# Even layer: the value sums of two query tiles of a head pair in one step behind the scores, and exponentials written over their arguments

## The chip, the cores and the metric

One core of a Trainium2 chip runs the whole kernel. The metric is the device time of one execution in microseconds (us); the median of the runs is given, with the lowest and the highest.

## The reference

The reference is a two-layer encoder over 256 tokens of 1024 features. Each layer is a mixer and a squared-ReLU MLP, each behind an RMS norm and with a residual. The even layer's mixer has two groups of 8 heads, which share an input projection and an output projection:

```python
hcat = xn @ w_in
out_a = neighbourhood_attention(...)        # 8 heads of 64, bias rpb, windows of a 64-wide grid
...
out_b = dense_attention(q, k, v, (MLA_NOPE + MLA_ROPE) ** -0.5)   # 8 heads, queries and keys of 96, values of 64
return jnp.concatenate([out_a, out_b], axis=-1) @ w_o
```

For each head and each query, both compute the softmax of the scores against all 256 keys and the weighted sum of the values. The odd layer (three dilated windows) and the MLPs are untouched by the change.

## The kernel before

Tokens are two tiles of 128 queries (`NT = 2`). Products that need full precision are made of three matmuls each (`mm3`, lines 208 to 211): an operand is split into a rounded high part, which ScalarE writes (`split`, line 205), and the remainder, which VectorE writes (line 206).

In the even layer, attention is cut into 16 items, in the order neighbourhood heads, then latent heads: for each pair of heads `hp` the query tiles `t = 0` and `t = 1`. So items 2·hp and 2·hp+1 are the two tiles of one pair of heads. An item passes through three steps.

- `scores(n)` (line 773) starts the load of a bias for item n+2, makes the scores of one query tile against 256 keys for two heads on TensorE (`two_heads`, line 218, for the neighbourhood heads, with weights of 64 rows x 128 columns; `mm3` with 96 rows for the latent heads), and computes the softmax: VectorE writes the negated arguments `sn` and their minima (line 791 or 794), ScalarE the exponentials `pp` and their sums (line 796), VectorE the reciprocals (line 797), ScalarE scales `pp` (line 799).
- `turn_probs(n)` (line 802) transposes `pp` in four pieces of 128x128 on TensorE (line 806), and copies the result to `pts` (line 808) on ScalarE or VectorE, whichever the framework takes.
- `mix(n)` (line 810) multiplies `pts` by the values on TensorE: 8 matmuls with weights of 128 rows x 64 columns (line 820), and splits the 128x128 result into the inputs of the output projection, `oah`/`oal` or `obh`/`obl` (lines 205 and 206).

`sn`, `pp` and `pts` come from one ring of 12 scratch buffers, which other parts of the kernel use as well.

The work around these steps is the `main` list: the projections of queries and keys, and, when those are through, the output projection into four open accumulators (`out_steps`; the last two of its eight parts are in `out_last`, behind the list). Each main step has a cost written by hand; the costs, less 5 at the start, add up to 36.3 units. The list of the attention's steps (`attention`, line 824) is spread over these units evenly, by its length:

```python
        for c, f in main:
            f()
            at += c
            while done < len(side) and done * total < at * len(side):
                side[done]()
                done += 1
```

Before the change the list has 50 entries, of which two are empty. From item 2 on its order is `scores(n)`, `turn_probs(n-1)`, `mix(n-2)`, and each is an entry of its own.

The order in which the steps are issued is a priority. The framework's scheduler fixes each engine's order ahead of the run; it keeps to the priorities as long as it expects an instruction's inputs in time, and otherwise lets later ones pass. What an engine is then given, it does in that order.

Weights come from HBM through SyncE's queue (line 151) into four raw buffers, in an order written out ahead (`specs`); the bias loads (line 771) stand in the same queue. Behind the even layer, `hand_over` adds the accumulators to the residual (line 308) and prepares the MLP's input `xx` (lines 245 and 246).

Of the kernel before, what the change touches and what calls it, by code (L numbers as in the profile page):

```python
# [26 lines left out]
P = 128  # L27
D = 1024
KT = D // P
T = 256  # L30
NT = T // P
# [18 lines left out]
def trunk(ctx, tc, a, out):  # L50
    nc = tc.nc
# [8 lines left out]
    def scratch(shape, name):  # L60

        n = int(np.prod(shape))
        v = work.tile([P, 512], F32, tag="scratch", name=name, bufs=12)[:, :n]
        if len(shape) == 2:
            v = v.rearrange("p (a b) -> p a b", b=shape[1])
        return v
# [8 lines left out]
    def quarter_pair(name):  # L75
        return [act.tile([P, KT // 2, T], F32R, tag="quarter", name=name + v, bufs=4) for v in "hl"]

    def bank(tag):
        return ps.tile([P, 512], F32, tag=tag, name=tag)
# [124 lines left out]
    def split(hi, lo, src, eng=None):  # L204
        a = nc.scalar.copy(hi, src).ins  # L205
        return a, (eng or nc.vector).tensor_tensor(lo, src, hi.bitcast(F32), op=ALU.subtract).ins  # L206

    def mm3(o, sh, sl, mh, ml, first, last):
        nc.tensor.matmul(o, sh, mh, start=first, stop=False)  # L209
        nc.tensor.matmul(o, sh, ml, start=False, stop=False)  # L210
        nc.tensor.matmul(o, sl, mh, start=False, stop=last)  # L211

    def two_heads(o, hi, lo, ts):

        for n, (y, z) in enumerate(((hi, hi), (hi, lo), (lo, hi))):
            for j in range(2):
                pb = slice(64 * j, 64 * j + 64)
                nc.tensor.matmul(o[j], y[pb, 0, ts], z[pb, 1, :], start=n == 0, stop=n == 2)  # L218
# [10 lines left out]
    def tok(t):  # L229
        return slice(t * P, (t + 1) * P)  # L230
# [323 lines left out]
    def even(ep):  # L554
# [208 lines left out]
        mixed = [quarter_pair("oa"), None]  # L763
        items = [(0, t, hp) for hp in range(4) for t in range(NT)] + [(1, t, hp) for hp in range(4) for t in range(NT)]
        biases, probs, turned = {}, {}, {}

        def load_bias(n):
            if n < 8:
                _, t, hp = items[n]
                biases[n] = ep.tile([P, 2, T], F32, tag="bias", name="bias", bufs=2)  # L770
                nc.sync.dma_start(biases[n], a["rpb"][t, hp])

        def scores(n):
            kind, t, hp = items[n]
            load_bias(n + 2)

            sb = [bank("w")[:, 0:T] for _ in range(2)] if kind == 0 else bank("w").rearrange("p (j n) -> p j n", j=2)
            s_of = lambda j: sb[j] if kind == 0 else sb[:, j]
            if kind == 0:
                two_heads(sb, *qk[hp], tok(t))  # L780
            else:
                for j in range(2):
                    h = 2 * hp + j
                    (qh, ql), (kh, kl) = mT["q"], mT["k"]
                    mm3(sb[:, j], qh[0:96, h, tok(t)], ql[0:96, h, tok(t)], kh[0:96, h, :], kl[0:96, h, :], True, True)
            pp, sn = scratch([2, T], "pp"), scratch([2, T], "sn")
            mn, z, rz = (work.tile([P, 2], F32, tag=v, name=v, bufs=3) for v in ("mn", "z", "rz"))
            for j in range(2):
                o = s_of(j)
                if kind == 0:  # L790
                    nc.vector.tensor_tensor_reduce(out=sn[:, j], in0=o, in1=biases[n][:, j, :], op0=ALU.add, op1=ALU.min,
                                                   scale=-1.0, scalar=3e38, accum_out=mn[:, j:j + 1])
                else:
                    nc.vector.tensor_scalar(sn[:, j], o, -MLA_SCALE, None, ALU.mult, ALU.min, accum_out=mn[:, j:j + 1])
            for j in range(2):
                nc.scalar.activation(pp[:, j], sn[:, j], AF.Exp, bias=mn[:, j:j + 1], scale=-1.0, accum_out=z[:, j:j + 1])
            nc.vector.reciprocal(rz, z)
            for j in range(2):
                nc.scalar.activation(pp[:, j], pp[:, j], AF.Copy, scale=rz[:, j:j + 1])
            probs[n] = pp  # L800
# [7 lines left out]
            nc.any.tensor_copy(out=turned[n], in_=pt.rearrange("p (b n) -> p b n", b=4))  # L808

        def mix(n):  # L810
            kind, t, hp = items[n]
            pts = turned.pop(n)
            if mixed[kind] is None:
                mixed[kind] = quarter_pair("ob")
            v = (vna, vml)[kind]
            pvo = bank("acc" if n < 6 else "w")
            for kk in range(NT):
                for j in range(2):
                    h = 2 * hp + j
                    nc.tensor.matmul(pvo[64 * j:64 * j + 64, 0:P], v[:, kk, h * 64:(h + 1) * 64], pts[:, 2 * j + kk, :],  # L820
                                     start=kk == 0, stop=kk == NT - 1)
            split(*(z[:, hp, tok(t)] for z in mixed[kind]), pvo[:, 0:P])

        def attention():

            out = []
            for n in range(len(items) + 2):
                for fn, m in ((scores, n), (turn_probs, n - 1), (mix, n - 2)):
                    if 0 <= m < len(items):
                        out.append(lambda fn=fn, m=m: fn(m))  # L830
                if n == 0:
                    out += [lambda: None] * 2
            return out
# [21 lines left out]
        main += [(0, lambda: accs.extend(open_accs()))]  # L855
        main += [(1.3, f) for k in range(6) for f in out_steps(accs, mixed, wo, k)]
        side = attention()
        at = -5
        total = sum(c for c, _ in main) + at
# [296 lines left out]
```

## Time and profile before

| what | value |
|---|---|
| median of 3 runs | 737.01 us (734.08 to 737.18) |
| the profiled execution: its time | 735.7 us |
| its span, first to last instruction | 733.9 us |
| its granted TensorE clock, mean | 0.997 of full speed |
| TensorE matmuls busy | 99% of the span |
| TensorE weight loads busy | 90% |
| VectorE busy | 85% |
| ScalarE busy | 71% |

Busy time counts a matmul from its start to its modelled end, and matmuls overlap, so 99% doesn't say how densely they stand. For that, one reads the distance from one start to the next. In the rows, PE is TensorE's matmuls, PEld its weight loads, DVE VectorE, ACT ScalarE, SPq SyncE's queue.

### The profile page before, as it was taken

To read this page: it belongs to the slowest core of one execution; us is meant where nothing else is said; L and a number is where in the kernel's file an instruction comes from. 1 tells how busy PE (TensorE), PEld (TensorE's weight loads), DVE (VectorE), ACT (ScalarE), POOL (GpSimd) and SP (SyncE) were. 2 spreads that over 40 slices of the span, in tenths; PEclk is the share of its full clock that TensorE was granted. 3 is DMA by queue.
4 is the path that set the end of the run, shared out by engine and by line. 5 is a ranking of instruction groups with operands and counts; after the bars stand their busy time and mean duration, and the time that the engine had idled before them with its cause. 6 is when DMAs were issued, how large, how long until landed. Compare 5 with 4: busy or idle time off the path is not lost.

```text
span 733.9 us, 13862 instructions
## 1 busy us (share of the span) xinstructions
PE 723.2 (99%) x5234; PEld 660.5 (90%) x5234; DVE 623.0 (85%) x1182; ACT 522.5 (71%) x991; POOL 118.4 (16%) x157
## 2 busy tenths in 40 slices
PE   9999999999999999999999999999999999999995
PEld 6988899999999998989899899898999999999984
DVE  6888859999999959878878887787859999999956
ACT  7778968767766756877776767767759766866751
POOL 0100002224222000012213212032103232212000
PEclk9999999999999999999999999999999999999998
DMA  8773338798899644663565555555658799888601
GB/s 314 272 260 138 116 115 215 213 291 241 262 264 241 215 155 166 218 217 126 201 215 184 175 189 184 175 187 202 226 182 214 223 287 258 247 239 252 204 11 57
DMA packets 36867, 149.56 MB, mean 204 GB/s; under 512 B 5120, under 2 KB 6656, under 8 KB 27712
## 3 DMA queue, kind: packets, MB, share of 16 engines
q1 hardware_dynamic: 26208, 128.20, 49.4%
q0 software_dynamic: 10304, 20.19, 15.1%
q8 instruction: 41, 0.67, 0.4%
q10 hardware_dynamic: 288, 0.28, 0.1%
q14 instruction: 26, 0.21, 0.1%
HBM read 142.10 MB, written 1.05 MB: 195 GB/s over the span
## 4 chain that ended last, share of the span: by engine, by line
PE 92%; DVE 4%; issue 1%; ACT 1%; DMA 0%; POOL 0%; POOLq 0%; SPq 0%; ACTq 0%; DVEq 0%
PE w L209 11%; PE w L210 11%; PE w L211 11%; PE acc L209 11%; PE acc L927 11%; PE acc L210 11%; PE acc L211 11%; PE acc L928 5%; PE w L1004 1%; PE w L218 1%; PE w L806 1%; PE acc L1019 1%; DVE wlo L206 1%; PE w L820 1%; DVE xx L246 1%
## 5 line engine op out<-in xcount | busy, mean ns | idle before, releaser
L206 DVE TENSOR_TENSOR wlo<-raw,whi 128x512 fp32r<-128x512 f32 (+3 forms) x360 | 297.8, 850 | 41.3 <-ACT whi L205 41.2
L205 ACT CAST whi<-raw 128x512 fp32r<-128x512 f32 (+3 forms) x360 | 253.9, 747 | 90.0 <-PE w L210 71.0
L210 PE MATMUL w<-xx,whi 128*128 128x256 f32 x528 | 149.6, 283 | 0.4 <-DVE xx L246 0.3
L211 PE MATMUL w<-xx,wlo 128*128 128x256 f32 x528 | 149.3, 283 | 0.0
L209 PE MATMUL w<-xx,whi 128*128 128x256 f32 x528 | 148.8, 283 | 0.0
L927 PE MATMUL acc<-xx,whi 128*128 128x512 f32 x336 | 122.0, 403 | 0.0
L210 PEld LDWEIGHTS w<-xx,whi 128*128 128x128 f32 x528 | 101.2, 192 | 1.9 <-DVE xx L246 0.8
L209 PEld LDWEIGHTS w<-xx,whi 128*128 128x128 f32 x528 | 101.0, 192 | 1.1
L211 PEld LDWEIGHTS w<-xx,wlo 128*128 128x128 f32 x528 | 101.2, 192 | 0.0
L928 PE MATMUL acc<-xx,wlo 128*128 128x256 f32 x336 | 94.3, 281 | 0.0
L144 POOL COPY sum<-sum 128x512 f32<-128x512 f32 x28 | 40.3, 1455 | 244.3 <-DMA sum<-in_w 150.2
L927 PEld LDWEIGHTS acc<-xx,whi 128*128 128x128 f32 x336 | 63.1, 188 | 14.1
L942 POOL DMA_DIRECT2D sw<-qk x84 | 41.4, 500 | 176.7 <-DVE qk L935 167.4
L928 PEld LDWEIGHTS acc<-xx,wlo 128*128 128x128 f32 x336 | 63.5, 189 | 0.0
L209 PE MATMUL acc<-whi,xx 128*128 128x384 f32 (+2 forms) x160 | 55.7, 350 | 0.1
L210 PE MATMUL acc<-wlo,xx 128*128 128x384 f32 (+2 forms) x160 | 55.4, 346 | 0.0
L211 PE MATMUL acc<-whi,xx 128*128 128x384 f32 (+2 forms) x160 | 54.9, 343 | 0.0
L209 PE MATMUL w<-whi,hh 128*128 128x512 f32 (+1 forms) x108 | 42.1, 390 | 0.0
L210 PE MATMUL w<-wlo,hh 128*128 128x512 f32 (+1 forms) x108 | 41.5, 384 | 0.0
L211 PE MATMUL w<-whi,hl 128*128 128x512 f32 (+1 forms) x108 | 41.2, 382 | 0.0
L205 ACT CAST hh<-h 128x896 fp32r<-128x896 f32 (+1 forms) x32 | 28.9, 903 | 14.3 <-DVE h L382 14.2
L206 DVE TENSOR_TENSOR suml<-sum,sumh 128x1024 fp32r<-128x1024 f32 x28 | 35.3, 1259 | 0.0
(233 smaller groups left out, 1576.7 us busy)
## 6 DMA issues: line engine op xcount, KB each, us to landing
raw<-in_w SPq DMA_DIRECT2D x36, 1024.0 KB, 5.2
raw<-in_w_oqk SPq DMA_DIRECT2D x24, 1024.0 KB, 4.9
raw<-in_w SPq DMA_DIRECT2D x28, 768.0 KB, 4.9
sum<-in_w POOLq DMA_DIRECT2D x28, 512.0 KB, 8.8
raw<-in_w_ov SPq DMA_DIRECT2D x16, 768.0 KB, 4.4
sum<-in_w SPq DMA_DIRECT2D x28, 256.0 KB, 6.3
sw<-qk POOLq DMA_DIRECT2D x84, 64.0 KB, 3.2
raw<-in_w_oe SPq DMA_DIRECT2D x4, 1024.0 KB, 5.0
```

Of the source, the lines that this page charges most:

```text
L144: nc.gpsimd.tensor_copy(out=sums[:, 1, :], in_=sums[:, 0, :])
L205: a = nc.scalar.copy(hi, src).ins
L206: return a, (eng or nc.vector).tensor_tensor(lo, src, hi.bitcast(F32), op=ALU.subtract).ins
L209: nc.tensor.matmul(o, sh, mh, start=first, stop=False)
L210: nc.tensor.matmul(o, sh, ml, start=False, stop=False)
L211: nc.tensor.matmul(o, sl, mh, start=False, stop=last)
L218: nc.tensor.matmul(o[j], y[pb, 0, ts], z[pb, 1, :], start=n == 0, stop=n == 2)
L246: lambda: nc.vector.scalar_tensor_tensor(lo, v, gk, hi.bitcast(F32), ALU.mult, ALU.subtract).ins)
L806: nc.tensor.transpose(pt[:, b * P:(b + 1) * P], pp[:, b // 2, (b % 2) * P:(b % 2 + 1) * P], ident)
L927: nc.tensor.matmul(two(pq), wh[:, ws], xT[:, :, k, :], start=k == 0, stop=False)
L928: nc.tensor.matmul(pq[:, T:2 * T], wl[:, ws], xh[:, k, :], start=False, stop=k == KT - 1)
L942: swap = (lambda o, i: nc.gpsimd.dma_start(o, i)) if wide else nc.scalar.copy
```

## The change

`scores` keeps the negated arguments and the exponentials in one buffer. `mix` is called once for two items, with the odd one's number: it takes the transposed probabilities of both query tiles, makes 16 matmuls into one bank of 256 columns, and splits 128x256 at once. In the attention's list, `mix(n-2)` is no longer an entry of its own: for odd n it stands in the entry of `scores(n)`, right behind it and ahead of `turn_probs(n-1)`. The list has 35 entries then, two of them empty.

```diff
-            pp, sn = scratch([2, T], "pp"), scratch([2, T], "sn")
+            pp = sn = scratch([2, T], "pp")
...
         def mix(n):
-            kind, t, hp = items[n]
-            pts = turned.pop(n)
+
+            kind, _, hp = items[n]
             if mixed[kind] is None:
                 mixed[kind] = quarter_pair("ob")
             v = (vna, vml)[kind]
             pvo = bank("acc" if n < 6 else "w")
-            for kk in range(NT):
-                for j in range(2):
-                    h = 2 * hp + j
-                    nc.tensor.matmul(pvo[64 * j:64 * j + 64, 0:P], v[:, kk, h * 64:(h + 1) * 64], pts[:, 2 * j + kk, :],
-                                     start=kk == 0, stop=kk == NT - 1)
-            split(*(z[:, hp, tok(t)] for z in mixed[kind]), pvo[:, 0:P])
+            for t in range(NT):
+                pts = turned.pop(n - 1 + t)
+                for kk in range(NT):
+                    for j in range(2):
+                        h = 2 * hp + j
+                        nc.tensor.matmul(pvo[64 * j:64 * j + 64, tok(t)], v[:, kk, h * 64:(h + 1) * 64], pts[:, 2 * j + kk, :],
+                                         start=kk == 0, stop=kk == NT - 1)
+            split(*(z[:, hp, :] for z in mixed[kind]), pvo[:, 0:T])
 
         def attention():
 
             out = []
             for n in range(len(items) + 2):
-                for fn, m in ((scores, n), (turn_probs, n - 1), (mix, n - 2)):
-                    if 0 <= m < len(items):
-                        out.append(lambda fn=fn, m=m: fn(m))
+
+                now = [(scores, n)] + [(mix, n - 2)] * (n % 2 and n > 2)
+                for step in (now, [(turn_probs, n - 1)]):
+                    step = [(fn, m) for fn, m in step if 0 <= m < len(items)]
+                    if step:
+                        out.append(lambda step=step: [fn(m) for fn, m in step])
                 if n == 0:
                     out += [lambda: None] * 2
             return out
```

## Rows read from the trace of the kernel before

**Rows 1.** The page's first part: busy time, share of span, instructions of each engine.
```profile
PE 723.2 (99%) x5234; PEld 660.5 (90%) x5234; DVE 623.0 (85%) x1182; ACT 522.5 (71%) x991; POOL 118.4 (16%) x157
```

**Rows 2.** Busy time by stretch: window, length, each engine's busy us, clock, DMA, GB/s.
```profile
38.00:112.00 74.00, 74.00 (x629) 65.42 (x628) 57.45 (x175) 59.20 (x164) 3.07 (x6) 1.00 0.44 153
...
60.00:82.00 22.00, 22.00 (x178) 18.84 (x177) 20.03 (x67) 20.41 (x60) 0.89 (x3) 1.00 0.19 61
```

**Rows 3.** Waits of the weight loads, 38 to 112 us: total us, times, longest.
```profile
PEld w L820 <- DVE sn L794: 0.5, 3, 0.2
```

**Rows 4.** Timeline of PE, item 15's sum: start us, us, line, tiles, shape, count.
```profile
107.68 0.28 PE L210 MATMUL acc<-obl,whi 128*128 128x256 f32 x1
...
108.88 0.28 PE L211 MATMUL acc<-obh,wlo 128*128 128x256 f32 x1
109.08 0.66 PE L820 MATMUL w<-pts,vml 128*64 128x128 f32 x8
...
109.89 0.28 PE L210 MATMUL acc<-obl,whi 128*128 128x256 f32 x1
```

**Rows 5.** The same sum in narrow windows, from its second and third pair.
```profile
109.25 0.49 PE L820 MATMUL w<-pts,vml 128*64 128x128 f32 x5
...
109.35 0.39 PE L820 MATMUL w<-pts,vml 128*64 128x128 f32 x4
```

**Rows 6.** Timeline of PE: item 1's sum beside item 4's scores.
```profile
52.95 0.28 PE L211 MATMUL acc<-xx,wlo 128*128 128x256 f32 x1
53.16 0.66 PE L820 MATMUL acc<-pts,vna 128*64 128x128 f32 x8
...
54.51 0.28 PE L210 MATMUL acc<-xx,whi 128*128 128x256 f32 x1
```

**Rows 7.** Timeline of PE: item 1's scores alone, between projections.
```profile
42.93 0.28 PE L211 MATMUL acc<-xx,wlo 128*128 128x256 f32 x1
...
43.91 0.28 PE L210 MATMUL acc<-xx,whi 128*128 128x256 f32 x1
```

**Rows 8.** Timeline of PE: latent scores of item 13 behind the output projection.
```profile
93.23 0.28 PE L211 MATMUL acc<-oah,wlo 128*128 128x256 f32 x1
93.36 0.28 PE L209 MATMUL w<-kh,qh 96*128 96x256 f32 x1
```

**Rows 9.** Timeline of PE: item 8's sum, whose first piece has two matmuls.
```profile
83.51 0.43 PE L820 MATMUL w<-pts,vml 128*64 128x128 f32 x2
```

**Rows 10.** Timelines: transposes of items 15 and 7, and the copies that follow them.
```profile
106.34 0.60 PE L806 MATMUL w<-ident,pp 128*128 128x128 f32 x4
...
106.97 0.59 ACT L808 COPY pts<-w 128x512 f32<-128x512 f32 x1 [0.95 <-PE w L806]
...
72.85 0.60 PE L806 MATMUL w<-ident,pp 128*128 128x128 f32 x4
...
77.11 0.68 DVE L808 COPY pts<-w 128x512 f32<-128x512 f32 x1
```

**Rows 11.** Groups by line, 38 to 112 us: shapes, count, busy us, mean ns, idle.
```profile
L205 ACT CAST obh<-w 128x128 fp32r<-128x128 f32 x8 | 2.1, 261 | 0.9 <-PE w L820 0.8
...
L752 ACT COPY ktok<-acc 128x256 f32<-128x256 f32 x4 | 1.4, 359 | 0.0
...
L206 DVE TENSOR_TENSOR obl<-w,obh 128x128 fp32r<-128x128 f32 x8 | 2.3, 288 | 3.6 <-ACT obh L205 3.5
...
L754 DVE COPY vml<-acc 128x256 f32<-128x256 f32 x4 | 1.7, 420 | 0.4 <-ACT ktok L752 0.3
```

**Rows 12.** The chain that ended last, at the layer's end: start us, us, what.
```profile
109.08 1.06 ACT whi L205
...
111.38 0.20 DVE obl L206
...
119.23 0.39 PE w L210
```

**Rows 13.** Timeline of SyncE's queue: start us, time the issue took, count.
```profile
62.98 40.52 SPq L151 DMA_DIRECT2D raw<-in_w  x5
```

## The prediction

> **What bounds the kernel.** I read the page's busy shares first: TensorE's matmuls fill 99% of the span, VectorE 85%, ScalarE 71% [rows 1]. As overlapping matmuls flatter that share, I then read the changed stretch, 38 to 112 us, by windows: TensorE never shows a gap there, while VectorE and ScalarE have 16.6 and 14.8 us to spare of 74, though in its middle, 60 to 82 us, only 2.0 and 1.6 of 22 [rows 2]. The waits say how much TensorE stands still for others: its longest wait for another engine ahead of a sum of values is 0.5 us in all [rows 3]. So in this stretch the time is the number of TensorE's starts, times their distances; the work of the other engines costs nothing as long as it is in time. That makes the timeline of TensorE's starts the view that decides.
>
> **The distances.** Plain 256-column matmuls start 0.12 us apart: 1.20 us from 107.68 to 108.88 with ten steps [rows 4]. The pairs of a sum start about 0.11 apart once it runs [rows 5]. From the last matmul ahead of the sum of item 15 to the second behind it are 109.89 − 108.88 = 1.01 us [rows 4]. Two plain steps and four pairs would be 0.24 + 0.44 = 0.68. The other 0.33 us is the way in and out: the array goes from weights of 128x128 to 128x64 and back, the first start comes late, the one after it too, and the same again behind the sum.
>
> Scores of neighbourhood heads have such a price as well: 43.91 − 42.93 = 0.98, less 0.24 and three pairs of 0.12, is 0.38 [rows 7]. Where sum and scores stand side by side they share: 54.51 − 52.95 = 1.56, less 0.24, 0.44 and 0.36, is 0.52 [rows 6]. There the sum adds only 0.52 − 0.38 = 0.14. The latent heads' scores, with 96 rows, have no such price: they start 0.13 behind the matmul ahead [rows 8]. So a sum beside them pays its 0.33.
>
> The timeline has 17 pieces of sums in the 16 items, as item 8's is in two [rows 9]: 3 beside neighbourhood scores, 14 not. That is 3 × 0.14 + 14 × 0.33 = 5.04 us.
>
> **What the change does to that.** *Half as many sums.* The matmuls stay as many; a joined sum is 0.44 + 0.44 long and pays its way in and out once. There are 8. Three stand behind neighbourhood scores (items 1, 3 and 5, behind the scores of 3, 5 and 7), five elsewhere: 3 × 0.14 + 5 × 0.33 = 2.07 us. Gain 5.04 − 2.07 = 2.97 us, all of it on TensorE, the engine that bounds. The trace has sums ahead of scores and none behind them; the price there lies between 0 and 0.33, and I take 0.14, as it is the same passage the other way round. If all three cost 0.33 the gain is 2.40.
>
> *Joined sums may come apart.* The scheduler parted item 8's, where one copy was late [rows 9]. Each parting gives back 0.33. I count one of the eight; the bounds are none and all eight, which would leave 0.33 of the gain.
>
> *Splits of 256 columns.* ScalarE's part takes 0.26 us at 128 columns and 0.36 in the nearest copy of 256; VectorE's 0.29 and 0.42 [rows 11]. Eight pairs give 8 × (0.52 − 0.36) = 1.3 us on ScalarE and 8 × (0.58 − 0.42) = 1.3 on VectorE. TensorE hides both, so I count nothing; should the cover go, they are a gain in any case. The Trainium skill, in TensorEngine Tiling (Array Packing), section PSUM Bottleneck, holds that small array forms speed up TensorE but not the reading of its results, and advises to read several tiles of a bank at once. By that rule the gain would be these 1.3 us in place of the 2.97; the short waits of TensorE speak against it here [rows 3].
>
> *Exponentials in place.* No instruction is added or removed; ScalarE reads and writes the same elements in order. Sixteen buffers fewer are drawn from the ring of 12, while the copy of an even item is held until its partner's sum. Nothing on TensorE waited visibly for this ring: no cost, no gain. If buffers became short instead, the copies would be late, which is the rival below.
>
> *The steps' places.* With 35 entries over 36.3 units in place of 50, an entry comes every 1.04 units, not 0.73; a main step of 1.3 units is 12 × 0.12 = 1.44 us. Scores of item 2 move from 3.6 to 5.2 units, those of 15 from 31.9 to 32.2. The bias loads, issued with the scores, move with them, up to 1.8 us later, and the weight loads behind them in SyncE's queue too. That queue spreads the next five weight loads over 40.5 us [rows 13]: it waits for free buffers and is far ahead. No cost; without that lead it would be the 1.8 us at most. GpSimd's queue has nothing of these steps.
>
> *The end of the layer.* The last sum now holds two items: 0.44 us longer, and its split by 0.10 and 0.13. From there the chain goes over VectorE to the next layer's first products at 119.23 [rows 12], so lateness there is not hidden by itself. But the split waited between two weight splits anyway, 0.20 us of it on the chain. Bounds: 0 and 0.67. I take 0.2, nearer to the row's 0.13 of VectorE.
>
> **The sum.** 2.97 − 0.33 − 0.2 = 2.4 us less. The profiled execution took 735.7 (span 733.9 and 1.8 around it), which gives 733.3; the median of the runs shown is 1.3 higher, 737.0, which gives **734.6 us**. That is 0.33% less, under the 0.5% (3.7 us) that a measurement of this kernel can tell from no change.
>
> **Rivals.** *TensorE waits behind the scores* (slower). The sum of an odd item used to come about four entries behind its transposes; now it comes one entry and the scores behind them. By the costs in the code, that is between scores alone (item 13: 0.44 + six matmuls, 0.72, = 1.2 us) and a main step more (2.6). A prompt copy lands 107.56 − 106.34 = 1.2 us after its transposes start, but item 7's landed 77.79 − 72.85 = 4.9 after them, in the crowded middle [rows 10]. There the new distance is 0.44 + about 1.1 + 0.72 = 2.3: 2.6 us late. One such wait nearly cancels the gain; two are 5.2 us, giving 734.6 + 5.2 = 739.8. From 2.4 us of waits on, the change loses. For it: the 2.0 and 1.6 us of room in the middle. Against: the scheduler lets other matmuls pass a sum that it expects late, as in item 8, and both engines have 1.3 us less to do. The Trainium skill, in TensorE: Matmul & The Clock Gate, section Part 3: Packing small matmuls, has it that matmuls run strictly in order; by that rule all that stands behind a waiting sum waits too. Chance 0.12.
>
> *The joining does not reach TensorE.* If the scheduler parts most sums, or moves them away from the scores, the gain shrinks to between 0.33 and 1.3, less 0.2 at the end: about 736.4. For it: one of 16 was parted in a stretch with the copies four entries ahead. Chance 0.18.
>
> *The end of the layer takes it back.* If the next products wait for VectorE's chain, and it starts later by all of 0.67 us plus one weight split of 1.2 that slips ahead, 1.9 us of 2.6 go: 736.3. The gap that the chain shows at its end speaks for it, VectorE's idle time ahead of 109 us against. Chance 0.10.
>
> *More than counted.* If the lighter middle also mends later places in the fixed order, 1 to 2 us come on top: 733. The waits show nothing to mend [rows 3]. Chance 0.10.
>
> **How the numbers follow.** The forecast has the other 0.50, with its own range of 733.4 to 735.4 (no parting and no end cost, 2.97, and up to a slack of 1.6, with the three passages at full price and the end at its bound). The range takes in the rivals between and much of the slower one, and the runs' own 3 us of scatter: 731.8 to 738.6. Faster by over 0.5% is below 733.3: part of the last rival and of the forecast's scatter, 0.15. Slower, above 740.7: the slower rival with more than two waits, 0.06. Same: 0.79.
>
> **What would show it.** Right: 128 matmuls at line 820 as before, but in 8 blocks of 16; about 1.45 us from the matmul ahead of a block to the second one behind it; 8 roundings and 8 subtractions fewer, those left at 256 columns; no wait at line 820 over 0.5 us; the last sum's end about 2.5 us earlier. Wrong: more than 11 blocks; idle time ahead of line 820 of 2.4 us or more; or the last sum earlier but the first products of the next layer not.

## The result, and where the time went

The changed kernel takes 737.21 us, the median of 20 executions (734.99 to 738.50); the kernel before, on the same chip, 735.25 (734.08 to 738.31, 20 executions). The ratio is 1.0021, with an interval of 1.0012 to 1.0030: some 1.5 us more, where 2.4 us less had been forecast. The profiled execution of the changed kernel took 736.64 us, with a span of 734.8 and a mean granted clock of 0.996.

**The even layer does what was forecast.** The page's first part of the changed kernel stands against [rows 1]: nine VectorE and seven ScalarE instructions fewer, as many matmuls.

```profile
PE 720.8 (98%) x5234; PEld 660.2 (90%) x5234; DVE 619.2 (84%) x1173; ACT 520.9 (71%) x984; POOL 123.5 (17%) x157
```

The windows of the stretch (columns as in [rows 2]) show TensorE without a gap, as before, and 17 more starts of matmuls within the same 74 us:

```profile
38.00:112.00 74.00, 74.00 (x646) 67.50 (x645) 56.89 (x168) 58.66 (x158) 3.48 (x7) 1.00 0.46 158
60.00:82.00 22.00, 22.00 (x183) 19.10 (x180) 19.35 (x65) 20.24 (x57) 0.59 (x2) 1.00 0.18 61
```

The timeline of TensorE in the changed kernel at its last sum answers to [rows 4] (the sum is line 822 now):

```profile
106.01 0.28 PE L211 MATMUL acc<-obh,wlo 128*128 128x256 f32 x1
106.22 1.09 PE L822 MATMUL w<-pts,vml 128*64 128x128 f32 x16
107.24 0.39 PE L209 MATMUL acc<-obh,whi 128*128 128x256 f32 x1
107.47 0.28 PE L210 MATMUL acc<-obl,whi 128*128 128x256 f32 x1
```

From the matmul ahead to the second one behind are 107.47 − 106.01 = 1.46 us, and the matmul behind the sum starts at 107.24, not at 109.67. Five of the eight joined sums stand whole like this one. The other three are parted, one of them into three pieces, as the same view shows in the crowded middle:

```profile
64.39 0.66 PE L822 MATMUL acc<-pts,vna 128*64 128x128 f32 x8
...
67.75 0.43 PE L822 MATMUL acc<-pts,vna 128*64 128x128 f32 x2
...
69.24 0.65 PE L822 MATMUL acc<-pts,vna 128*64 128x128 f32 x6
```

That makes 12 pieces in place of 17. Among the next layer's first products TensorE is ahead: the matmul that started at 122.11 us starts at 119.60. Of these 2.5 us it had 0.3 already where the layer begins (39.74 in place of 40.08); the layer itself is 2.2 shorter.

**The lead is lost at one place, 60 us later.** Counting matmuls from the end, the lead is the same for each up to the one that started at 180.34 in the kernel before. The timelines of TensorE at this place, before and then after:

```profile
180.34 0.39 PE L211 MATMUL acc<-sumh,hl 128*128 128x512 f32 x1
180.56 0.28 PE L209 MATMUL w<-xx,whi 128*128 128x256 f32 x1
```
```profile
177.83 0.39 PE L211 MATMUL acc<-sumh,hl 128*128 128x512 f32 x1
180.83 0.39 PE L209 MATMUL w<-xx,whi 128*128 128x256 f32 x1 [2.61 <-ACT relu L373]
```

A distance of 0.22 us has become 3.00. TensorE arrives 2.5 us early and leaves 0.27 late. This is the first MLP. The waits of the changed kernel from 150 to 182 us (columns: who waited for whom, total us, times, longest) name the chain:

```profile
POOL sum L144 <- DVE every L180: 10.1, 1, 10.1
DVE raw L179 <- issue: 7.3, 1, 7.3
...
PEld w L209 <- ACT relu L373: 3.0, 1, 3.0
PE w L209 <- ACT relu L373: 2.6, 1, 2.6
```

Read from below: TensorE waits for ScalarE's `relu`, and VectorE had stood idle for 7.3 us ahead of `raw` (line 179). "issue" means that the view found no releaser there; the timelines do. Here is GpSimd in the changed kernel, then in the kernel before (start, duration):

```profile
155.00 9.70 POOL L144 COPY sum<-sum 128x512 f32<-128x512 f32 x1 [10.12 <-DVE every L180]
165.00 1.09 POOL L145 DMA_DIRECT2D sum<-in_w  x1 [0.30 <-POOL sum L144]
```
```profile
151.93 0.61 POOL L144 COPY sum<-sum 128x512 f32<-128x512 f32 x1 [3.81 <-ACT hh L205]
...
163.01 1.32 POOL L144 COPY sum<-sum 128x512 f32<-128x512 f32 x1 [9.09 <-DMA sum<-in_w]
...
173.17 4.35 POOL L144 COPY sum<-sum 128x512 f32<-128x512 f32 x1 [7.45 <-DVE wlo L206]
```

The MLP's weights come in blocks that are also needed as sums. `load_weight` loads one block (line 143), GpSimd copies it (line 144), and a DMA from GpSimd's queue adds two other blocks to the pair (line 145). The copy takes 0.61 us when it runs freely; here it took 9.70. VectorE's timeline over the same time shows why its row stopped:

```profile
163.55 0.68 DVE L180 TENSOR_TENSOR every<-raw 128x512 f32<-128x512 f32 x1
171.51 0.69 DVE L179 TENSOR_TENSOR raw<-sum,raw 128x512 f32<-128x512 f32 x1 [7.28 <-issue]
```

VectorE ran without a pause until 164.23. It stopped because its next operation needs the block whose copy could not run beside it. Then the copy ended (164.70), the adding DMA went out at 165.00 and had landed by 171.51, and all that hangs on it (`wlo`, `relu`, TensorE's products) came late.

VectorE's row is itself another one. Counted from the end of the kernel, 16 of VectorE's places (121 to 159 us) and 13 of ScalarE's (121 to 149) hold another instruction than before. VectorE's timelines where the long difference begins, before and then after:

```profile
144.45 0.69 DVE L179 TENSOR_TENSOR raw<-sum,raw 128x512 f32<-128x512 f32 x1
145.05 1.22 DVE L206 TENSOR_TENSOR suml<-sum,sumh 128x1024 fp32r<-128x1024 f32 x1
```
```profile
142.94 1.10 DVE L179 TENSOR_TENSOR raw<-sum,raw 128x512 f32<-128x512 f32 x1
143.96 1.22 DVE L206 TENSOR_TENSOR wlo<-raw,whi 128x1024 fp32r<-128x1024 f32 x1
```

So: 2.5 us gained, 2.8 lost. In this profile another 0.65 us went in the odd layer, at a transpose that waited 0.9 us, behind a late transfer; e3, the same kernel, doesn't have that. What probably makes the difference of the medians as large as it is, e3 shows. The chain that ended last (the page's fourth part) has the shift in its shares: 92% for PE and none for POOL before, and now

```profile
PE 77%; DVE 9%; ACT 4%; DMA 4%; issue 3%; POOL 3%; SPq 0%; POOLq 0%; DVEq 0%; ACTq 0%
```

### The profile page after: what moved, and what is told of

Same layout as the page of the kernel before. It is cut to its first block, busy times and chain, and to the rows that moved or that the text cites. A ratio compares the mean times of both kernels' runs of the same rounds, so it can differ in the third digit from the quotient of the medians.

```text
span 734.8 us, 13840 instructions
## 1 busy us (share of the span) xinstructions
PE 720.8 (98%) x5234; PEld 660.2 (90%) x5234; DVE 619.2 (84%) x1173; ACT 520.9 (71%) x984; POOL 123.5 (17%) x157
## 4 chain that ended last, share of the span: by engine, by line
PE 77%; DVE 9%; ACT 4%; DMA 4%; issue 3%; POOL 3%; SPq 0%; POOLq 0%; DVEq 0%; ACTq 0%
PE acc L209 10%; PE w L209 9%; PE w L210 9%; PE acc L210 9%; PE acc L211 9%; PE w L211 9%; PE acc L932 8%; PE acc L933 4%; DVE wlo L206 4%; POOL sum L144 2%; DMA sum<-in_w 1%; PE w L218 1%; DMA sw<-qk 1%; ACT whi L205 1%; PE w L1009 1%
## 5 line engine op out<-in xcount | busy, mean ns | idle before, releaser
L206 DVE TENSOR_TENSOR wlo<-raw,whi 128x512 fp32r<-128x512 f32 (+3 forms) x360 | 294.8, 845 | 37.9 <-ACT whi L205 37.7
L144 POOL COPY sum<-sum 128x512 f32<-128x512 f32 x28 | 46.0, 1659 | 241.4 <-DMA sum<-in_w 164.9
L206 DVE TENSOR_TENSOR hl<-h,hh 128x896 fp32r<-128x896 f32 (+1 forms) x32 | 35.2, 1099 | 0.0
```

Of the source, the lines that this page charges most:

```text
L144: nc.gpsimd.tensor_copy(out=sums[:, 1, :], in_=sums[:, 0, :])
```

## The experiments

In the table, "layer" is the time between two starts on TensorE, those of the same two matmuls in every kernel (40.08 and 122.11 us in the profile of before); "place" is the distance between the two starts shown above (180.34 and 180.56).

| kernel | median, us | ratio to before | layer, us | place, us |
|---|---|---|---|---|
| before | 735.25 | | 82.03 | 0.22 |
| changed | 737.21 | 1.0021 [1.0012, 1.0030] | 79.85 | 3.00 |
| e1: changed, two loads, no copy | 734.32 | 0.9981 [0.9969, 0.9993] | 79.79 | 0.22 |
| e2: before, two loads, no copy | 735.84 | 1.0005 [0.9993, 1.0016] | 81.69 | 0.22 |
| e3: changed, profiled again | 738.51 (one) | | 79.80 | 2.98 |
| e5: changed, copy on ScalarE | 734.00 | 0.9987 [0.9975, 0.9999] | 79.71 | 0.23 |
| e6: joined sums alone | 739.61 | 1.0060 [1.0047, 1.0073] | 81.89 | 2.95 |
| e7: in place alone | 734.91 | 0.9998 [0.9985, 1.0010] | 81.04 | 0.22 |
| e8: before, 24 matmuls fewer | 734.82 | 1.0002 [0.9990, 1.0014] | 79.31 | 1.00 |
| e9: changed, two fillers | 733.29 | 0.9979 [0.9970, 0.9988] | 80.23 | 0.23 |
| e10: before, copy on ScalarE | 736.46 | 1.0022 [1.0009, 1.0035] | 81.78 | 0.23 |

Each ratio is to executions of the kernel before on the same chip, taken in turn with it (medians 735.62 for e1 to e3, 735.31 for e5 to e8, 734.86 for e9 and e10). The layer in the three profiles that have the sums as before (before, e2, e10) lies between 81.7 and 82.0, so a difference of 0.3 there means nothing.

**e1 and e2: the copy taken away.** The same edit in the changed kernel and, as control, in the kernel before: the block is loaded twice and not copied. The order on TensorE, VectorE and ScalarE stays.

```diff
-            nc.sync.dma_start(sums[:, 0, :], blocks[:, 3, :])
-            nc.gpsimd.tensor_copy(out=sums[:, 1, :], in_=sums[:, 0, :])
+            for half in range(2):
+                nc.sync.dma_start(sums[:, half, :], blocks[:, 3, :])
```

Expected of e1:

> The changed kernel, but the second half of the tile of summed weight blocks (line 144) is filled by a second load from HBM and no longer by GpSimd's copy. The orders of TensorE, VectorE and ScalarE are the same as in the changed kernel, instruction by instruction. Theory A (a copy of GpSimd is held up while VectorE works without a pause, the next weights come late for it, and TensorE waits 2.8 us at 178 us): without the copy the wait is gone, the first up-product of that step starts 2.5 us earlier than in the kernel before, and the time is 2.0 to 2.8 us under the kernel before (0.9962 to 0.9973). Theory B (the new order of the instructions around the end of the even layer is what costs, or the loads): the wait at about 178 us stays, and the time is that of the changed kernel, 1.0015 to 1.003 of the kernel before. The 28 loads more are 7.3 MB on 150; if they are felt, both come out up to 1 us later.

Expected of e2:

> The kernel before with the same second load in place of GpSimd's copy; its orders on TensorE, VectorE and ScalarE are the same as before. Theory A: the kernel before has few or short waits of this kind in most executions (its profiled one has none), so the time is 0 to 1 us less than before (0.9985 to 1.0), and the first experiment is 2.0 to 2.8 us faster than this one. Theory B: no difference to the kernel before, and the first experiment is slower than this one by 1 to 2 us.

The control did not move. In the changed kernel the wait is gone, as TensorE's timeline of e1 at the place shows,

```profile
178.00 0.39 PE L211 MATMUL acc<-sumh,hl 128*128 128x512 f32 x1
178.22 0.28 PE L209 MATMUL w<-xx,whi 128*128 128x256 f32 x1
```

and TensorE keeps its lead to the last matmul, which starts at 722.58 in place of 725.06. The ratio of the two ratios, 0.9981/1.0005, is 1.8 us less: the worth of the change with the copy out of the way. That is under what was expected (2.0 to 2.8), and the two intervals leave it wide, about 0.6 to 3.0.

**e3: the changed kernel once more.** Nothing edited.

Expected:

> The changed kernel as it is, one more profile. Theory A: a copy at line 144 of over 5 us again somewhere between 140 and 200 us, and a wait of TensorE of 1.5 to 3 us behind it; if this execution has none, TensorE's starts stay 2.5 us ahead of the kernel before through the whole first MLP. Theory B: a wait of the same length at the same matmul, whatever the copies at line 144 take.

The copy was held again, at 155.78 us, for 9.97 us. A second cost came behind it. The windows of e3 (length, busy us of PE, PEld, DVE, ACT, POOL, then the granted clock) show it:

```profile
175.00:180.00 5.00, 4.34 (x20) 3.23 (x18) 5.00 (x9) 1.13 (x2) 0.00 (x0) 1.00 0.75 213
180.00:185.00 5.00, 3.07 (x16) 3.08 (x17) 4.97 (x7) 5.00 (x7) 0.00 (x0) 0.75 0.73 262
185.00:190.00 5.00, 5.00 (x38) 4.87 (x37) 5.00 (x7) 2.06 (x4) 2.56 (x2) 0.91 0.51 152
```

After TensorE's wait the granted clock is 0.75 and 0.91 of full speed in two windows, a mix of its two levels of 2.4 and 1.2 GHz. The 24 matmuls behind the wait took 186.40 − 181.93 = 4.47 us, against 2.98 in the first profile of the same kernel, where the clock stayed at 1.00: 1.5 us more. The first profile was probably the rarer case. Of the 20 executions, 12 have a mean clock of 0.994 or 0.995, with a median of 737.5 us, and 8 of 0.996 or 0.997, with a median of 735.7. Of the 29 of the kernel before beside e5 to e8 only one lies below 0.996. The mean does not say where the clock fell: e1's profile has 0.995 without any fall at the place. Of the three profiles with the wait, e3 and e6 show the fall and the first does not. So the wait costs 2.8 us, and probably in most executions 1.5 more: 2.8 + 1.5 − 2.2 (the layer's gain) = 2.1, about the difference of the medians.

**e5 and e10: the copy on another engine.** Again the changed kernel and the control, with another way around GpSimd.

```diff
-            nc.gpsimd.tensor_copy(out=sums[:, 1, :], in_=sums[:, 0, :])
+            nc.scalar.copy(sums[:, 1, :], sums[:, 0, :])
```

Expected of e5:

> The changed kernel with the copy of the weight block on ScalarE in place of GpSimd (0.6 us each, beside the transfers as before). Theory A (VectorE's row of subtractions keeps GpSimd's copy out for some 10 us in the first MLP, and TensorE then waits 2.8 us for the late weights): no copy of over 1.5 us, no wait of TensorE over 1 us between 175 and 185 us, and 1 to 2.5 us less than the kernel before: 733.1 to 734.6. Theory B (the copies on GpSimd are late for another cause, or the time goes elsewhere): 736 to 737.5, as the changed kernel. Against A would also be a wait of the same size at the same matmuls with a copy of ordinary length. ScalarE's queue is the copy's place now, where it can wait for a load: a price of up to 1 us is possible in either theory.

Expected of e10:

> The kernel before with the copy of the weight block on ScalarE: the control of the changed kernel with the same edit (734.0). If that one's gain is the joined sums', with the held copy out of the way, this one stays within 0.7 us of the kernel before. If taking the copy off GpSimd is worth 1 us or more by itself, it falls to 734.3 or less and the changed kernel's version shows nothing of the sums.

With the sums joined the edit brings 2.5 us (0.9987 against 1.0021). Without, it costs 1.6 (734.86 to 736.46), more than was allowed for: TensorE waits for `relu` in the second MLP, 1.6 us in e10's profile (at 594.05) and 0.9 in e5's (at 591.48). ScalarE has a price of its own as the copy's place, but nothing holds the copy up there. The ratio of the ratios, 0.9987/1.0022, puts the change at 2.6 us. This pair shows less than e1 and e2, as the edit also gives VectorE and ScalarE another order through both MLPs, in either kernel.

**e6 and e7: the two halves of the change.** e6 is the changed kernel with two buffers again, e7 the kernel before with one.

```diff
-            pp = sn = scratch([2, T], "pp")
+            pp, sn = scratch([2, T], "pp"), scratch([2, T], "sn")
```
```diff
-            pp, sn = scratch([2, T], "pp"), scratch([2, T], "sn")
+            pp = sn = scratch([2, T], "pp")
```

Expected of e6:

> The joined sums with the exponentials in a buffer of their own, as before. If the part that writes over the arguments does nothing by itself, all is as in the changed kernel: 736 to 738.5, a copy of 8 us or more at about 155 us, TensorE's first products of the next layer 2.4 to 2.6 us earlier than in the kernel before, and a wait of 2 to 3 us at about 178 us. If sharing the buffer is what shifts VectorE's row against the copy, the copy stays below 5 us and the time falls to 733 to 734.5.

Expected of e7:

> The kernel before with only the exponentials written over their arguments. By the prediction it costs nothing: the time of the kernel before within 0.7 us, 17 pieces of sums as before, and TensorE's first products of the next layer within 0.2 us of where they were. If sharing the buffer by itself shifts the order on VectorE and ScalarE or makes a subtraction wait for its buffer: a shift of TensorE by 0.3 us or more within the even layer, or a copy held for 8 us or more at about 155 us with 1.5 to 3 us more time.

These were meant for the held copy alone, and they say more. e7 leaves the order of the MLP's rows as it was before, holds no copy for more than 3.5 us, and shortens the layer by 1.0 us: its item 8 isn't parted, so that 16 pieces stand for 17. By the prediction's price that piece is 0.33 us; the rest was not traced, and the median shows no gain (0.9998). e6 came out slower than either of its forecasts, and not ahead at the next layer's products. It holds the copy and loses at the place, as the changed kernel does; here are its GpSimd and TensorE timelines:

```profile
158.02 10.00 POOL L144 COPY sum<-sum 128x512 f32<-128x512 f32 x1 [8.09 <-ACT whi L205]
```
```profile
73.60 0.45 PE L209 MATMUL acc<-whi,ch 128*128 128x384 f32 x1 [0.46 <-DVE oal L206]
...
75.19 0.28 PE L712 MATMUL w<-ident,ktok 128*96 128x128 f32 x1 [0.27 <-ACT ktok L752]
...
184.29 0.58 PE L209 MATMUL w<-xx,whi 128*128 128x256 f32 x1 [2.57 <-ACT relu L373]
```

But the joined sums alone gain only 0.14 us in the layer, with the same 12 pieces. The first two lines show part of where it went, 0.73 us: TensorE waits for the subtraction that empties a joined sum's bank, and soon after for a copy. One group of the neighbourhood heads' scores is parted as well. The rest was not traced. Whole, the change gains 2.2; so the half with "no cost, no gain" is needed for the other one's gain. How sharing a buffer changes the order that the scheduler makes was not traced.

e6 also settles a rival: that TensorE, if it comes to the MLP early, merely waits there for a chain that runs at its own times. In e6 it comes 0.7 us later than in the kernel before (122.81 against 122.11), and loses the 2.7 us all the same.

**e8: the same lead by other means.** In the kernel before, the third product of the output projection is left out for slices 3 to 5, just ahead of the MLP.

```diff
-            mm3(o, w[0][:, cs], w[1][:, cs], m[0][v], m[1][v], first and fb % 2 == 0, last and fb % 2 == 1)
+            if third:
+                mm3(o, w[0][:, cs], w[1][:, cs], m[0][v], m[1][v], first and fb % 2 == 0, last and fb % 2 == 1)
+            else:
+                nc.tensor.matmul(o, w[0][:, cs], m[0][v], start=False, stop=False)
+                nc.tensor.matmul(o, w[0][:, cs], m[1][v], start=False, stop=False)
...
-            onto(accs, wo[k // 2], (k % 2) * D, (ALL, k % 4), mixed[k // 4], k == 0, k == KT - 1, fbs)
+            onto(accs, wo[k // 2], (k % 2) * D, (ALL, k % 4), mixed[k // 4], k == 0, k == KT - 1, fbs, not short or k < 3)
...
```

Expected:

> The kernel before without the third product (low part of the weights) of the even layer's output projection for its last three slices: 24 matmuls of 256 columns, 2.9 us of TensorE by 0.12 us each, just ahead of the MLP. It leaves that part of the computation out. Theory A (a copy held by VectorE, which depends on how VectorE's row happens to lie against it): TensorE is 2.9 us ahead at the next layer's first products, and either keeps it (732.5 to 733.5) where the copies are of ordinary length, or loses it in one wait where a copy is held for 8 us or more. Theory C (the MLP's chain of weights, transfers and splits comes at its own times, so that any earlier arrival of TensorE is waited off): a wait of 2 to 3 us between 175 and 185 us without a held copy, and 735 to 736, as the kernel before.

In between. GpSimd's and TensorE's timelines of e8:

```profile
153.83 6.28 POOL L144 COPY sum<-sum 128x512 f32<-128x512 f32 x1 [8.46 <-DVE every L180]
```
```profile
178.26 0.39 PE L209 MATMUL w<-xx,whi 128*128 128x256 f32 x1 [0.62 <-ACT relu L377]
```

A lead of 3.1 us ahead of the place loses 0.8 there to a copy held for 6.3 us, and more later; the last matmul is 1.6 earlier in the profile, and the median does not show even that. A few rows of the MLP stand in another order here too. So a lead gained ahead of the MLP in another way was given back in part as well; as the order differs too, e8 does not part the two.

**e9: the order put back.** The changed kernel, its GpSimd copies untouched, with two matmuls into an unused bank. They move the scheduler's expectations just so far that the MLP's rows come out as before, but for one pair on VectorE and one on ScalarE.

```diff
         main += [(1.3, f) for k in range(6) for f in out_steps(accs, mixed, wo, k)]
+
+        def fill():
+            o = bank("w")
+            for _ in range(2):
+                nc.tensor.matmul(o, warm[:, 0:P], warm, start=True, stop=True)
+        main += [(0, fill)]
```

Expected:

> The changed kernel, its copies on GpSimd as they are, with two matmuls of 512 columns into an unused bank behind the even layer's output projection (0.45 us of TensorE). With them the rows of VectorE and ScalarE in the first MLP stand in the order that they have in the kernel before, all but one pair of subtractions, while the sums stand as in the changed kernel, in 12 pieces. Theory A1 (the new order of those rows is what holds the copy): no copy of 8 us or more at about 155 us, no wait of TensorE over 1 us at about 178 us, TensorE 1.9 to 2.2 us ahead at the next layer's first products and 1.3 to 2.6 us at the end, and 733 to 734.4. Theory A2 (the joined sums, by coming to the MLP 2.5 us earlier, hold the copy in whatever order): a copy of 8 us or more, a wait of 2 to 3 us, and 736.5 to 738.

Here are e9's GpSimd timeline, then TensorE's at the place:

```profile
150.76 0.66 POOL L144 COPY sum<-sum 128x512 f32<-128x512 f32 x1 [3.72 <-DMA sum<-in_w]
...
161.78 1.44 POOL L144 COPY sum<-sum 128x512 f32<-128x512 f32 x1 [8.98 <-DVE wlo L206]
...
172.01 4.40 POOL L144 COPY sum<-sum 128x512 f32<-128x512 f32 x1 [7.40 <-DVE wlo L206]
```
```profile
178.70 0.39 PE L211 MATMUL acc<-sumh,hl 128*128 128x512 f32 x1
178.93 0.28 PE L209 MATMUL w<-xx,whi 128*128 128x256 f32 x1
```

The copies take about what they took before (0.61, 1.32 and 4.35) and there is no wait. TensorE is 1.6 us ahead at the next layer's first products, under the 1.9 expected, as it began the layer 0.2 late. With 733.29 us this is, by the ratio, the fastest version beside e1: 1.6 us less than before, with 0.45 of fillers still in it. So the joined sums and an early arrival alone do not hold the copy. e6 is the counterpart: a late arrival, with the changed kernel's order of VectorE and ScalarE from 121 us on, and the copy is held. What goes with the held copy is the order of the MLP's rows. Its profiled execution took 735.18, with its lead cut late in the odd layer; eight of the eleven took 733.06 to 733.42.

**e4 and e11: the copy beside VectorE, by itself.** Neither does any of the encoder's work.

Expected of e4:

> Not the encoder: a small kernel that does none of the reference's computation. It measures the disputed cost alone: GpSimd's copy of 128x512 is released while VectorE works through a train of 0, 2, 4, 8 and 16 subtractions with both inputs in SBUF, all ready at once, and then through 16 subtractions of 512 columns with one input in PSUM. Theory A: the copy alone takes 0.6 us, and beside the trains it ends only behind their last subtraction: about 1, 3.5, 8 and 17 us long. Theory B: 0.6 to 2 us whatever the train's length. For the PSUM train, A leaves it open whether one SBUF input is enough to hold the copy.

Here is e4's timeline: the copy, and VectorE's rows that it met (the last field counts the operations).

```profile
7.63 0.61 POOL L48 COPY dsta<-srca 128x512 f32<-128x512 f32 x1 [7.19 <-ACT srca L37]
...
16.12 8.44 DVE L47 TENSOR_TENSOR wd<-big,x 128x1024 f32<-128x1024 f32 x7
16.32 1.49 POOL L48 COPY dstd<-srcd 128x512 f32<-128x512 f32 x1 [2.94 <-ACT srcd L37]
...
25.08 17.11 DVE L47 TENSOR_TENSOR we<-big,x 128x1024 f32<-128x1024 f32 x15
25.28 17.38 POOL L48 COPY dste<-srce 128x512 f32<-128x512 f32 x1 [7.47 <-ACT srce L37]
...
43.36 9.66 DVE L42 TENSOR_TENSOR wf<-bank,gof 128x512 f32<-128x512 f32 x16 [1.17 <-ACT gof L36]
43.91 0.61 POOL L48 COPY dstf<-srcf 128x512 f32<-128x512 f32 x1 [1.24 <-ACT srcf L37]
```

Neither forecast came true as a whole. Alone the copy takes 0.61. Beside seven operations with two operands in SBUF it came in after the first; beside fifteen of the same kind it was held to the last. With one operand in PSUM (the last pair) it was not held at all.

Expected of e11:

> It does none of the reference's computation: 18 rows of some eleven VectorE operations each, back to back, and beside each row one GpSimd copy of 128x512 that can start in the row's second or third operation. Six rows of two-input operations of 1024 columns, six that alternate 1024 and 512, six of 1024 with one operation on a PSUM operand in the sixth place; within each six the second operation has 128 to 768 columns, so that the copy meets the row at another place. If VectorE's row holds the copy as a whole whenever it runs without a pause: 8 to 12 us in all of the first twelve. If the copy is let in at the boundaries between operations by chance of place: some of 0.6 to 2 us and some held to the row's end. In the last six, if an operation with a PSUM operand lets it in, no copy over 6 us.

```profile
21.31 10.30 POOL L51 COPY dstlong<-srclong 128x512 f32<-128x512 f32 x1 [12.82 <-ACT srclong L37]
...
34.92 1.29 POOL L51 COPY dstlong<-srclong 128x512 f32<-128x512 f32 x1 [3.31 <-ACT srclong L37]
...
164.81 4.50 POOL L51 COPY dstbank<-srcbank 128x512 f32<-128x512 f32 x1 [11.07 <-ACT srcbank L37]
...
168.75 0.68 DVE L47 TENSOR_TENSOR wbank<-bank,x 128x512 f32<-128x512 f32 x1
```

Of the first twelve copies six took 0.61 to 1.56 us and six 7.5 to 10.7, in strict turns. So beside operations that do not depend on each other the copy comes in at the first boundary, or not before the row pauses. In the last six rows the first copy came in at once; the other five took 4.5 to 5.0 us and ended at 169.31 and at like places, while the operation with the PSUM operand ran: it lets the copy in.

What decides at the first boundary stays open. In the first twelve rows the turns go with two things at once. The copies came in where the row's second operation has 128, 384 or 640 columns and were held at 256, 512 and 768; and they came in where VectorE had stood idle ahead of the row (1.17 us, in the first row 0.09) and were held where it had not. The last six rows speak against the columns, as 384 and 640 were held there as well (4.63 and 4.90 us). But the idle time can't be all: e4's row of seven also followed without a pause, and let the copy in.

In the encoder's own traces held copies also came in where VectorE did not pause. The 4.35 us copy of the kernel before ended at 177.52, here in VectorE's timeline:

```profile
176.37 0.68 DVE L179 TENSOR_TENSOR raw<-sum,raw 128x512 f32<-128x512 f32 x1
177.08 0.99 DVE L180 TENSOR_TENSOR every<-raw 128x512 f32<-128x512 f32 x1
```

`every` reads what `raw` has just written, and took 0.99 us in place of 0.68. The 6.28 us copy of e8 ended inside `hl`, which took 1.48 in place of 1.08. In the row that held the changed kernel's copy, `suml` stands between `raw` and `every`, and `hl` took 1.08. That may be how the order of the rows decides; no run tests it.

## Why the prediction was wrong

**The distances, half as many sums.** Right in kind: 1.46 us around a whole block (1.45 forecast), 128 matmuls, and no wait ahead of a sum over 0.5. By the prediction's prices 12 pieces, three of them beside neighbourhood scores, cost 3 × 0.14 + 9 × 0.33 = 3.39 us against 5.04. The price of a sum behind scores, guessed at 0.14, was 0.15: from the matmul ahead of the scores at 50.85 to the second behind the sum are 52.65 − 50.64 = 2.01 us, less 0.24, 0.36, 0.88 and the scores' 0.38.

**Joined sums may come apart.** Mis-sized: one parting was counted and there are four (12 pieces for 8 sums), 1.0 us less gain. The prediction's own sign of being wrong, more than 11 blocks, came.

**Exponentials in place: no cost, no gain.** Wrong. e7 has the layer 1.0 us shorter by this alone, and without it (e6) the joined sums gain nothing that can be measured. 5.04 − 3.39 + 1.0 = 2.6, and 2.2 were measured, where the halves alone gained 0.14 and 1.0. The forecast of 2.4 for the layer is near in part by luck: two of its terms were off in opposite directions, and the halves do not simply add up.

**Splits of 256 columns and the end of the layer.** As forecast: the subtraction of 256 columns took 0.42 us, TensorE hid it, and the next layer's products start 2.5 us earlier in the profile.

**The sum: the step that failed.** It carried the even layer's 2.4 us to the end of the kernel, as if the 600 us behind it stood still. "The steps' places" looked for GpSimd's part in the changed steps alone ("GpSimd's queue has nothing of these steps"), and of the rows that it rests on only [rows 12] reach beyond 112 us, apart from the whole run's totals [rows 1]. The scheduler makes one order for the whole kernel from what it expects; the change gave the rows of VectorE and ScalarE another order from 121 to 159 us, in code that the diff doesn't touch. One GpSimd copy then met VectorE's row where it could not get in, and 2.8 us were gone, 4.3 where the clock fell too (e3). Why that order keeps the copy out stays open.

**The rivals.** None named this place. "The end of the layer takes it back" has the right form, a lead that is lost where the next work hangs on VectorE, but in the wrong place and for another cause. The range (731.8 to 738.6) holds the result, and so does the likeliest class, within 0.5% either way; the direction was wrong. The forecast time itself was built on a median of three runs, 737.0, which lies 1.8 above that of the twenty.

**What the trace of before could have told.** Its GpSimd copies of 1.32 and 4.35 us beside others of 0.61 stood in the view. The Trainium skill, SBUF — State Buffer, section Who interferes with whom, names such a cause: VectorE and GpSimd share a pair of ports, a VectorE operation with two operands in SBUF against a GpSimd operation that reads SBUF is such a case, and the later one waits for the whole instruction. The traces agree on the kind of operation (e4's PSUM row does not hold the copy). They differ on the length: it is not one instruction of at most 1.2 us but 9.7, 10.0 and 17.4 us, in the changed kernel over eleven further instructions. By that section alone an estimate for this copy is one such instruction, 1.2 us more, which VectorE's and TensorE's room would have hidden; measured, it set the time.

## What to carry to other kernels

Where a scheduler fixes the orders, compare them over the whole kernel after a local edit, not only in the stretch that was edited: two filler matmuls moved the changed kernel by 0.4%, some 3 us. A small GpSimd copy on the way to a DMA is a risk beside a dense row of VectorE operations that read two operands from SBUF; load the block twice (e1), or see that the row is broken by an operation on PSUM (e11). And a gain on the bounding engine is only kept if each later place has that much room: e8 lost half of a lead, and the changed kernel all of it.

## What had not been expected of the hardware

The copy's wait, which is no fixed price: 0.61 to 1.56 us or 7.5 to 10.7, in strict turns, in e11's first twelve rows, 17.4 in e4, and up to 10.0 in the encoder. And the price of a wait of TensorE of some 2.6 us: in two of the three profiles that have it (e3, e6) the granted clock fell behind it, in e3 for 1.5 us on top (24 matmuls in 4.47 us against 2.98 in the first profile, where it stayed at 1.00).
